# Taking the last norm's memory ahead of the general path's, and issuing its vector's load from SyncE

## The chip, the cores and the metric

The kernel runs on one core of a Trainium2 chip. A core has a matrix engine (PE), a vector engine (DVE), a scalar engine (ACT), GpSimd (POOL) and a sync engine (SP) that issues most of the DMAs here. Each engine takes its instructions strictly in the order in which they stand in its own queue, and waits for others on semaphores. The metric is the device time of one execution in microseconds (us): the median of three runs of the kernel before is 693.87 us (692.81 to 694.31).

## What is computed

One decoder block over 256 tokens of 1024 features: attention and a convolution side by side, cross-attention into a memory, and then a mixture of 32 experts and a last norm. Only the end matters here:

```
x = x + hierarchical_moe(h, ...)      # per token: the 2 best experts of the best group of 8
    # each expert: (silu(t @ w_gate) * (t @ w_up)) @ w_down, weighted and summed
return rmsnorm(x, final_g)            # x * rsqrt(mean(x*x) + eps) * final_g
```

`w_gate` and `w_up` are 1024 x 512 and `w_down` 512 x 1024 float32 for each of 32 experts: 192 MB that all have to come from memory.

## The kernel before

The experts are taken four at a time, in eight groups (`for g in range(NGR)`). Each expert has 32 slots for tokens (`CAP`), four experts fill 128 partitions, and each of the four quarters of PE's columns works for one expert. For a group PE gathers the tokens (L1034), multiplies with `w_gate` into `eg` and with `w_up` into `eu` (`two_rows`, L1310, where the loads are cut fine, otherwise L1339). Then `hidden_T` makes the hidden rows: ACT applies silu to `eg` (L1051), DVE multiplies with `eu` (L1052), PE turns the result over (L1055), ACT copies it to `hT` (L1058). Then PE multiplies with `w_down` into `ed`, and the result is spread back to the tokens and summed in the four banks `Y`.

Weights go through a ring of memory units of 8 KB per partition (`Ring`). `ring.queue` lists all loads in order ahead of time; `ring.done` gives units back and `ring.pump` then issues the next loads, from SP (L139). `ring.spare` hands out a unit for something that isn't a listed load.

An expert may get more than 32 tokens, so there is a general path, `overflow`: the engines read a count, and a loop handles the surplus where there is one. In these inputs the loop isn't entered. It has loads of its own into four spare units, `ow`. Every DMA of the program reports on one of eight semaphores (DMAHW0 to DMAHW7), used in turn and counted upwards, and the loop's loads count too. Where the loop isn't entered SP therefore goes another way (L1119): for six of the eight semaphores, one after another, it waits until the loads issued so far on it have landed, and then adds what the loop's load would have added.

The last group (g = 7) ends in `finale`. Its `w_down` is cut by rows of the experts, j = 0 to 3, and by columns, so that the last products wait for little data. In order of issue: (j = 0, in two pieces of 1 MB), then columns 0 to 511 of j = 1, 2, 3 (1 MB each), columns 512 to 1023 of j = 1, 2 (1 MB each), and columns 512 to 767 and 768 to 1023 of j = 3 (0.5 MB each). `SLICES` names the three column slices n = 0, 1, 2. `finale` is written out by hand for PE, ACT and DVE (`manual_schedule`): `down` and `down_c` are the products with `w_down` (L1179), `slots` copies them out of the banks (ACT, L1189), `spread` adds them to the tokens (PE, L1185), `begun` puts x itself into a bank (PE, L1173). The norm: `square` and `square_v` (ACT L1193, DVE L1198 and L1199) sum the squares into `junk`, DVE multiplies slice 0 by the vector `final_g` (L1249), `add_part` (DVE L1204), `root` (ACT L1207) and two reciprocals (DVE L1263, L1270) give the factor, `scaled` and `scaled_a` apply it (DVE L1212, ACT L1219), and two stores follow (L1222, one from SP and one from ACT).

Behind the last group's product with `w_gate` the code takes the general path (`overflow(*table)`), and behind that the memory for the end: `fin["g"]` for the vector `final_g`, loaded from ACT (L1346), `fin["Z"]` for the output and `fin["junk"]` for the squares. `close_sum` then finishes the right halves of the sums (L1163, L1164).

Of the kernel before, what the change touches and what calls it, by code (L numbers as in the profile page):

```python
# [21 lines left out]
P = 128  # L22
# [164 lines left out]
def body(tc, a, out):  # L187
    nc = tc.nc
# [808 lines left out]
    def e_ps(name, shape=(P, 512)):  # L997
        return ps2.tile(list(shape), F32, tag="e", name=name)
# [7 lines left out]
    def pick_mats(key_v, n, eng, SR=None):  # L1006

        w = n // CAP
        Sv = mo.tile([P, NT, n], F32, tag="S", name="S")
        if SR is None:  # L1010
            SR = mo.tile([P, NT, n], F32, tag="SR", name="SR")
        V.tensor_tensor(Sv.rearrange("p i (q c) -> p i q c", c=CAP),
                        iota1.unsqueeze(1).unsqueeze(1).to_broadcast([P, NT, w, CAP]),
                        key_v.unsqueeze(3).to_broadcast([P, NT, w, CAP]), op=OP.is_equal)
        A.activation(SR[:, 0], Sv[:, 0], AF.Copy, scale=r2[:, 0:1])  # L1015
        last_pick[0] = eng.tensor_scalar(SR[:, 1], Sv[:, 1], r2[:, 1:2], None, op0=OP.mult)  # L1016
        return Sv, SR

    def gate_mats(Sv, g_v, n):

        Sq = Sv.rearrange("p i (q c) -> p i q c", c=CAP)
        V.tensor_tensor(Sq, Sq, g_v.unsqueeze(3).to_broadcast([P, NT, n // CAP, CAP]), op=OP.mult)  # L1022
        return Sv
# [4 lines left out]
    def gather(SR, n, tg, j0=0, j1=NJ, step=4):  # L1028

        for ja in range(j0, j1, step):  # L1030
            t = e_ps("tgp", (P, step, n))
            for j in range(step):
                for i in range(NT):
                    T.matmul(t[:, j], X[:, i, ja + j::NJ], SR[:, i], start=i == 0, stop=i == NT - 1)  # L1034
            V.tensor_tensor(tg[:, ja:ja + step], t,  # L1035
                            gff[:, ja:ja + step].unsqueeze(2).to_broadcast([P, step, n]), op=OP.mult)

    def put_back(GS, n, GST=None):
        t = e_ps("GSp", (P, NT, P))
        for i in range(NT):  # L1040
            T.transpose(t[0:n, i], GS[:, i], ident)
        if GST is None:
            GST = mo.tile([n, NT, P], F32, tag="SR", name="GST")
        V.tensor_copy(GST, t[0:n])
        return GST
# [18 lines left out]
    def combine(pd, n, GST, yd, outs, w, first=False, last=False):  # L1064

        ins = A.copy(yd[:, :w], pd[0:n, :w])  # L1066
        for i in range(NT):
            T.matmul(outs[i], GST[:, i], yd[:, :w], start=first, stop=last)  # L1068
        return ins
# [45 lines left out]
    def overflow(ntot, eidx, thr):  # L1115

        ow, slots = zip(*[ring.spare((SLOT,)) for _ in range(4)])
        nv = nc.values_load(ntot[0:1, 0:1], min_val=0, max_val=NITEM)
        with tc.If(nv > 0):  # L1119
            with tc.For_i(0, nv, 1) as it_:  # L1120
                er = nc.values_load(eidx[0:1, ds(it_, 1)], min_val=0, max_val=NE - 1)
                kv = mo.tile([P, NT, 1], F32, tag="kc", name="okv")
                gv = mo.tile([P, NT, 1], F32, tag="gc", name="ogv")
                V.tensor_copy(kv, key[:, :, ds(er, 1)])
                V.tensor_copy(gv, GT[:, :, ds(er, 1)])
                V.tensor_tensor(kv, kv, thr[:, ds(it_, 1)].unsqueeze(1).to_broadcast([P, NT, 1]), op=OP.subtract)
                small_ = ow[2]
                Sv, SR = pick_mats(kv, CAP, G, small_[:, 0:NT * CAP].rearrange("p (i t) -> p i t", i=NT))
                tg = small_[:, 1280:1280 + NJ * CAP].rearrange("p (j t) -> p j t", j=NJ)
                gather(SR, CAP, tg)  # L1130
                GST = put_back(gate_mats(Sv, gv, CAP), CAP,
                               small_[0:CAP, 256:256 + NT * P].rearrange("p (i t) -> p i t", i=NT))
                pgu = []
                for w in (w_gate, w_up):
                    o = e_ps("oo")
                    for h in range(2):
                        wt_ = ow[h].rearrange("p (j f) -> p j f", j=4)
                        nc.sync.dma_start(wt_, w[ds(er, 1)].rearrange("o (p j) f -> p (o j) f", j=NJ)[:, 4 * h:4 * h + 4])
                        for jj in range(4):
                            j = 4 * h + jj  # L1140
                            T.matmul(o[0:CAP], tg[:, j], wt_[:, jj], start=j == 0, stop=j == NJ - 1,
                                     tile_position=(0, 0))
                    pgu.append(o)
                hh = hidden_T(pgu[0], pgu[1], CAP, small_[0:CAP, 512:512 + DE],
                              small_[:, 1024:1024 + 4 * CAP].rearrange("p (j t) -> p j t", j=4))
                yd = ow[3][0:CAP, 0:D].rearrange("p (n f) -> p n f", n=2)
                for n in range(2):
                    o = e_ps("od")
                    wt_ = ow[n].rearrange("p (j f) -> p j f", j=4)
                    nc.sync.dma_start(wt_, w_down[ds(er, 1)].rearrange("o (p j) n -> p (o j) n", j=4)[  # L1150
                        :, :, 512 * n:512 * n + 512])
                    for j in range(4):
                        T.matmul(o[0:CAP], hh[:, j], wt_[:, j], start=j == 0, stop=j == 3, tile_position=(0, 0))
                    combine(o, CAP, GST, yd[:, n], Ycols(512 * n, 512), 512)
        ring.done(*slots)


    fin = {}

    def close_sum():  # L1160

        for i in range(NT):
            T.matmul(Yp[i][1], ident, X[:, i, 512:], start=False, stop=True)  # L1163
            V.tensor_copy(X[:, i, 512:], Yp[i][1])  # L1164
# [158 lines left out]
    table = None  # L1323
    for g in range(NGR):
        tg, GS = state
        GST = put_back(GS, P) if g > 0 else None
        pgu = []
        for kind in ("eg", "eu"):
            o = e_ps(kind)
            if (kind, g) == ("eg", 0):  # L1330
                first_gate(o, tg)
            elif (kind, g) in FINE:
                for m in range(4):
                    two_rows(kind, g, m, o, tg)
            else:
                ws = [ring.take((kind, g, q)) for q in range(4)]
                for j in range(NJ):
                    for q in range(4):
                        T.matmul(o[32 * q:32 * q + 32], tg[:, j, 32 * q:32 * q + 32], ws[q][0][:, j],  # L1339
                                 start=j == 0, stop=j == NJ - 1, tile_position=(0, 32 * q))  # L1340
                ring.done(*[units for _, units in ws])
            pgu.append(o)
            if (kind, g) == ("eg", NGR - 1):
                overflow(*table)
                fin["g"] = ring.spare((D,))[0]
                nc.scalar.dma_start(fin["g"], a["final_g"].partition_broadcast(P))  # L1346
                fin["Z"] = ring.spare((NT, D))[0]
                fin["junk"] = ring.spare((NT, D))[0]
                close_sum()
        GST = GST or put_back(GS, P)  # L1350
        hh = hidden_T(pgu[0], pgu[1], P)
        last = g == NGR - 1
        if g == 1:

            for i in range(NT):
                T.matmul(Yp[i][0], ident, X[:, i, 0:512], start=False, stop=False)
        if last:
            finale(g, hh, GST)
            break
        yd = new_yd(P)  # L1360
        os_ = [e_ps("ed") for _ in range(2)]
        ws = [[ring.take(("ed", g, q, h)) for h in range(1 if q < 2 else 2)] for q in range(4)]
        for j in range(4):
            for n in range(2):
                for q in range(4):
                    w = ws[q][0][0][:, j] if q < 2 else ws[q][j // 2][0][:, j % 2]
                    T.matmul(os_[n][32 * q:32 * q + 32], hh[:, j, 32 * q:32 * q + 32], w[:, 512 * n:512 * n + 512],  # L1367
                             start=j == 0, stop=j == 3, tile_position=(0, 32 * q))
        ring.done(*[units for wq in ws for _, units in wq])
        for n in range(2):  # L1370
            combine(os_[n], P, GST, yd[:, n], Ycols(512 * n, 512), 512, g == 0, False)
        if g == 0:
            table = overflow_table()
        state = start_group(g + 1)
# [28 lines left out]
```

## Time and profile before

| | us |
|---|---|
| median of 3 runs | 693.87 (692.81 to 694.31) |
| the profiled execution: its own time | 692.93 |
| the profiled execution: its span, first to last instruction | 691.2 |
| PE busy | 574.6 (83%) |
| DVE busy | 223.4 (32%) |
| ACT busy | 173.3 (25%) |
| POOL busy | 119.0 (17%) |
| moved by DMA | 237.34 MB, mean 343 GB/s |

The profile is one execution. Times in its views are microseconds from the span's start; an instruction is named by engine, source line, operation and what it writes from what it reads. A "q" behind an engine's name (ACTq, SPq) means its instruction sequencer: waits and DMA issues, which don't count as busy. In brackets stands how long the engine was idle before, and what ended that.

### The profile page before, as it was taken

The page shows a single profiled execution, that of the slowest core. Times are in us where ns is not written, and L with a number is a line of the kernel's source. Part 1 is how long each engine was busy: PE and PEld are TensorE (multiplying, and loading weights), DVE is VectorE, ACT ScalarE, POOL GpSimd, SP SyncE. Part 2 cuts the span into 40 slices and gives each one's busy share as a digit, 9 for nine tenths or more (in the row PEclk, how much of TensorE's full clock was granted, in tenths as well). Part 3 has the DMA queues.
Part 4 walks back from the last instruction along what each step waited for, and adds up shares of the span by engine and source line. Part 5 has one row for each costly group of instructions (what it writes and reads, how often), then busy time and mean ns, then how long its engine had stood idle before and what let it go on. Part 6 is the DMA issues. An engine that isn't in the chain of part 4 may idle for free. (4 is left out here: it accounts for less than half of the span.)

```text
span 691.2 us, 8710 instructions
## 1 busy us (share of the span) xinstructions
PE 574.6 (83%) x3497; PEld 343.7 (50%) x3497; DVE 223.4 (32%) x488; ACT 173.3 (25%) x377; POOL 119.0 (17%) x106
## 2 busy tenths in 40 slices
PE   7999999998999999979767947967894795788726
PEld 4989889877998753615212501511250161234202
DVE  5799789887674710400000100000010010001002
ACT  6575765573555601000001000000000000000004
POOL 4556435673434100000000000000000000000000
PEclk9999999999999999999979968987996998799958
DMA  7999503554847899999999999999999999999981
GB/s 257 298 254 366 214 31 122 183 195 172 323 157 280 351 415 416 429 420 429 430 419 429 427 427 423 424 428 422 431 425 429 421 428 425 422 429 408 404 313 61
DMA packets 58730, 237.34 MB, mean 343 GB/s; under 512 B 10796, under 2 KB 30400, under 8 KB 46656
## 3 DMA queue, kind: packets, MB, share of 16 engines
q1 hardware_dynamic: 58400, 235.72, 86.0%
q10 hardware_dynamic: 288, 1.05, 0.4%
q8 instruction: 28, 0.46, 0.3%
q14 instruction: 14, 0.11, 0.0%
HBM read 235.70 MB, written 1.05 MB: 343 GB/s over the span
## 5 line engine op out<-in xcount | busy, mean ns | idle before, releaser
L433 POOL TENSOR_TENSOR WL<-w,WH 128x512 fp32r<-128x512 f32 (+1 forms) x80 | 109.1, 1373 | 109.8 <-ACT WH L431 98.8
L1339 PE MATMUL eu<-w,tg 128*32 128x512 f32 x448 | 82.2, 717 | 44.5 <-DMA w<-in_w_up 44.5
L1367 PE MATMUL ed<-w,hT 128*32 128x512 f32 x448 | 74.3, 659 | 23.4 <-DMA w<-in_w_down 18.6
L431 ACT CAST WH<-w 128x512 fp32r<-128x512 f32 (+1 forms) x120 | 72.9, 619 | 47.8 <-PE pmk L438 8.3
L1016 POOL TENSOR_SCALAR SR<-S,r 128x128 f32<-128x128 f32 x7 | 4.2, 604 | 387.9 <-PE Y L1068 337.0
L1339 PEld LDWEIGHTS eu<-w,tg 128*32 128x32 f32 x448 | 17.9, 127 | 104.5 <-DMA w<-in_w_up 63.9
L1034 PEld LDWEIGHTS tgp<-SR,X 128*128 128x128 f32 x256 | 62.0, 335 | 12.0 <-ACT SR L1015 9.5
L1034 PE MATMUL tgp<-SR,X 128*128 128x128 f32 x256 | 63.8, 406 | 3.6 <-ACT SR L1015 3.6
L1052 DVE TENSOR_TENSOR sgm<-sgm,eu 128x512 f32<-128x512 f32 x8 | 5.5, 687 | 182.1 <-PE eu L1339 168.4
L534 DVE SCALAR_TENSOR_TENSOR cacc<-z,pT,cacc 128x256 f32<-128x256 f32 x116 | 56.4, 486 | 2.6
L1367 PEld LDWEIGHTS ed<-w,hT 128*32 128x32 f32 x448 | 19.1, 115 | 73.6 <-issue 41.1
L1339 PE MATMUL eg<-w,tg 128*32 128x512 f32 x384 | 50.4, 614 | 4.1 <-DMA w<-in_w_gate 4.1
L1058 ACT COPY hT<-hTp 128x512 f32<-128x512 f32 x8 | 4.7, 586 | 161.2 <-PE hTp L1055 129.2
L1022 DVE TENSOR_TENSOR S<-S,GT 128x256 f32<-128x256 f32 x8 | 3.4, 425 | 122.3 <-POOL SR L1016 122.2
L433 DVE TENSOR_TENSOR WL<-w,WH 128x512 fp32r<-128x512 f32 (+1 forms) x40 | 36.4, 912 | 10.7 <-ACT WH L431 10.4
L1051 ACT ACTIVATE sgm<-eg 128x512 f32<-128x512 f32 x8 | 4.8, 597 | 135.2 <-PE eg L1339 85.6
L1339 PEld LDWEIGHTS eg<-w,tg 128*32 128x32 f32 x384 | 12.9, 112 | 37.1 <-issue 27.6
L1066 ACT COPY yd<-ed 128x512 f32<-128x512 f32 x14 | 8.2, 586 | 89.6 <-PE ed L1367 89.6
L1035 DVE TENSOR_TENSOR tg<-tgp,g_norm_ffn_g 128x512 f32<-128x512 f32 (+2 forms) x19 | 11.5, 607 | 53.0 <-PE tgp L1034 53.0
L1068 PE MATMUL Y<-yd,GST 128*128 128x512 f32 x56 | 25.9, 605 | 0.0
L1179 PE MATMUL ed<-w,hT 128*32 128x256 f32 (+1 forms) x96 | 9.2, 534 | 14.8 <-ACT hT L1058 14.8
L437 PE MATMUL pmk<-w,WH 128*128 128x256 f32 x64 | 18.7, 293 | 0.0
(354 smaller groups left out, 1005.3 us busy)
## 6 DMA issues: line engine op xcount, KB each, us to landing
w<-in_w_up SPq DMA_DIRECT2D x28, 2048.0 KB, 34.3
w<-in_w_gate SPq DMA_DIRECT2D x24, 2048.0 KB, 29.5
w<-in_w_down SPq DMA_DIRECT2D x35, 1024.0 KB, 31.5
w<-in_w_down SPq DMA_DIRECT2D x14, 2048.0 KB, 28.9
w<-in_w_gate SPq DMA_DIRECT2D x16, 1024.0 KB, 14.0
w<-in_w_mkv SPq DMA_DIRECT2D x8, 1024.0 KB, 12.9
w<-in_w_up SPq DMA_DIRECT2D x8, 1024.0 KB, 29.7
w<-in_w_in SPq DMA_DIRECT2D x7, 1024.0 KB, 7.3
```

The lines of the kernel that those rows point to most:

```text
L431: A.copy(hi, src)
L433: (V if nsplit[0] % 3 == 0 else G).tensor_tensor(lo, src, hi.bitcast(F32), op=OP.subtract)
L437: T.matmul(o, L[0], R[0], start=first, stop=False)
L534: V.scalar_tensor_tensor(dst, z[:, cb, t:t + S], pT[:, 4 * t + cb:4 * t + cb + 1], acc, op0=OP.mult, op1=OP.add)
L1034: T.matmul(t[:, j], X[:, i, ja + j::NJ], SR[:, i], start=i == 0, stop=i == NT - 1)
L1035: V.tensor_tensor(tg[:, ja:ja + step], t, gff[:, ja:ja + step].unsqueeze(2).to_broadcast([P, step, n]), op=OP.mult)
L1052: V.tensor_mul(sg, sg, pu[0:n])
L1066: ins = A.copy(yd[:, :w], pd[0:n, :w])
L1068: T.matmul(outs[i], GST[:, i], yd[:, :w], start=first, stop=last)
L1179: T.matmul(os_[n][32 * q:32 * q + 32, :w], hh[:, j, 32 * q:32 * q + 32], wq(q), start=j == 0, stop=j == 3, tile_position=(0, 32 * q))
L1339: T.matmul(o[32 * q:32 * q + 32], tg[:, j, 32 * q:32 * q + 32], ws[q][0][:, j], start=j == 0, stop=j == NJ - 1, tile_position=(0, 32 * q))
L1367: T.matmul(os_[n][32 * q:32 * q + 32], hh[:, j, 32 * q:32 * q + 32], w[:, 512 * n:512 * n + 512], start=j == 0, stop=j == 3, tile_position ...
```

## The change

`overflow(*table)` moves from ahead of the three `ring.spare` calls to behind them, and the load of `final_g` goes from ACT's queue to SP's:

```diff
             if (kind, g) == ("eg", NGR - 1):
-                overflow(*table)
                 fin["g"] = ring.spare((D,))[0]
-                nc.scalar.dma_start(fin["g"], a["final_g"].partition_broadcast(P))
+                nc.sync.dma_start(fin["g"], a["final_g"].partition_broadcast(P))
                 fin["Z"] = ring.spare((NT, D))[0]
                 fin["junk"] = ring.spare((NT, D))[0]
+                overflow(*table)
                 close_sum()
```

So the three units are taken from those that are free before the general path takes its four, and none of them is a unit into which the general path loads. The load's line becomes L1345.

On ACT, where the general path's branch (L1119) is behind it and `hidden_T` of the last group comes next (`hT` is the hidden rows, `hTp` the bank they come from; DMAHW0 to 7 are the DMAs' semaphores, the number behind them is a serial number of the program):

```order
 L1119 UNCONDITIONAL_BRANCH [waits Activation_49,Activation_sequencer_49]
-L1346 DMA w<-in_final_g 128x1024 [waits DMAHW2_49,DMAHW4_49,DMAHW0_49,PE_49]
 L1058 COPY hT<-hTp 128x512 [waits DVE_49,PE_49]
 L1189 COPY yd<-ed 128x512 [waits PE_49,Activation_49]
 L1240 ACT_TABLE_LOAD
```

The load, with its waits for three DMA semaphores, is gone from the place ahead of the copy to `hT`; the copy's own waits are for DVE and PE alone, in both kernels.

On SP, at the end of the list of loads and ahead of the read of the general path's count (`ntot`):

```order
 L139 DMA w<-in_w_down 128x4x256 [waits DMAHW2_49]
 L139 DMA w<-in_w_down 128x4x256 [waits DMAHW3_49]
+L1345 DMA w<-in_final_g 128x1024 [waits DMAHW4_49]
 L1118 TENSOR_LOAD ntot [waits DVE_49]
 L1119 COMPARE_AND_BRANCH
```

The load now stands behind the last two pieces of `w_down` and ahead of the branch, and waits for one semaphore, the one that it will report on itself: DMAHW4, used last by the load eight places before it.

On DVE, where the last norm begins (the first read of `final_g`, which is `w` here):

```order
 L1052 TENSOR_TENSOR sgm<-sgm,eu 128x512 [waits DVE_49,PE_49,Activation_49]
-L1249 TENSOR_TENSOR w<-Y_3019,w 128x512 [waits DMAHW2_49,DMAHW4_49,DMAHW0_49,Activation_49]
+L1249 TENSOR_TENSOR w<-Y_3019,w 128x512 [waits DMAHW4_49,DMAHW2_49,DMAHW7_49,DMAHW1_49,Activation_49]
 L1249 TENSOR_TENSOR w<-Y_3021,w 128x512 [waits Activation_49]
 L1204 SCALAR_TENSOR_TENSOR fpart<-fss,eps_t 128x1 x2
```

The order is the same; the multiplication waits for the vector in both kernels (DMAHW4), and for earlier users of its output's unit, which is another one now. PE's and POOL's orders are the same in both kernels.

## Rows read from the trace of the kernel before

**Rows 1.** The page: span, and the DMA engines' busy share in 40 slices
```profile
span 691.2 us, 8710 instructions
...
DMA  7999503554847899999999999999999999999981
```

**Rows 2.** The chain that ended last, window 640 to 692 (start, length, what)
```profile
668.82 0.04 ACTq L1346
...
670.02 3.64 PE ed L1179 x24
```

**Rows 3.** Timeline of ACT, 600 to 692
```profile
636.79 0.60 ACT L1051 ACTIVATE sgm<-eg 128x512 f32<-128x512 f32 x1 [18.09 <-PEq L1119]
...
669.38 0.59 ACT L1058 COPY hT<-hTp 128x512 f32<-128x512 f32 x1 [31.99 <-DMA w<-in_w_down]
```

**Rows 4.** Line L1346 alone: count, durations in ns, first and last start
```profile
L1346 ACTq EVENT_SEMAPHORE  x2: 17/28/38, 637.7 to 668.8; - x2
...
DMA to landing us min/median/max: 4.0/4.0/4.0
```

**Rows 5.** Line L1119 on SP, in windows 663.1 to 666.5 and 668 to 668.73
```profile
L1119 SPq EVENT_SEMAPHORE  x2: 17/17/17, 663.5 to 666.0; - x2
...
L1119 SPq EVENT_SEMAPHORE  x1: 17/17/17, 668.7 to 668.7; - x1
```

**Rows 6.** Timeline of PE, 640 to 692
```profile
654.53 0.64 PE L1055 MATMUL hTp<-ident,sgm 128*128 128x128 f32 x4
670.02 3.64 PE L1179 MATMUL ed<-w,hT 128*32 128x512 f32 x24 [14.85 <-ACT hT L1058]
673.59 1.11 PE L1173 MATMUL yl<-X,ident 128*128 128x256 f32 x2
674.63 3.65 PE L1179 MATMUL ed<-w,hT 128*32 128x512 f32 x40
678.20 1.98 PE L1185 MATMUL Y<-yd,GST 128*128 128x512 f32 x4
...
680.55 1.93 PE L1179 MATMUL ed<-w,hT 128*32 128x256 f32 x32
```

**Rows 7.** Line L139 on SP, window 636.5 to 638.8: one load of `w_down`
```profile
L139 SPq DMA_DIRECT2D w<-in_w_down x1: 2308/2308/2308, 636.5 to 636.5; - x1
...
DMA to landing us min/median/max: 18.6/18.6/18.6
```

**Rows 8.** DMA by queue (q1 SP, q10 ACT), windows 670:671, 671:672, 672:673
```profile
q1 hardware_dynamic: 128, 0.12, 38.7%
...
q10 hardware_dynamic: 74, 0.27, 76.0%
q1 hardware_dynamic: 3, 0.00, 0.7%
...
q10 hardware_dynamic: 16, 0.03, 7.6%
```

**Rows 9.** Timeline of SP, 560 to 692
```profile
634.16 28.21 SPq L139 DMA_DIRECT2D w<-in_w_down  x9
```

**Rows 10.** Stretches: PE, PEld, DVE, ACT, POOL busy, PEclk, DMA share, GB/s
```profile
657.00:670.00 13.00, 0.00 (x0) 0.00 (x0) 0.00 (x0) 0.59 (x1) 0.00 (x0) 0.51 0.99 356
670.00:674.00 4.00, 3.98 (x25) 1.40 (x26) 0.00 (x0) 0.00 (x0) 0.00 (x0) 0.50 0.46 162
674.00:688.00 14.00, 10.48 (x88) 4.72 (x87) 4.59 (x15) 7.14 (x18) 0.00 (x0) 0.98 0.06 25
```

**Rows 11.** Timeline of DVE, 637 to 692
```profile
680.15 1.49 DVE L1249 TENSOR_TENSOR w<-Y,w 128x512 f32<-128x512 f32 x2 [26.08 <-ACT w L1193]
681.55 0.22 DVE L1204 SCALAR_TENSOR_TENSOR fpart<-fss,eps_t 128x1 f32<-128x1 f32 x2
683.79 0.16 DVE L1204 SCALAR_TENSOR_TENSOR fpart<-fss,fpart 128x1 f32<-128x1 f32 x1 [2.02 <-ACT w L1193]
```

## The prediction, made before the changed kernel ran

> **What bounds the kernel now.** I read the DMA share in slices first: from the middle of the span to its last two slices the DMA engines are 90% busy or more [rows 1], so most of the kernel runs at the rate at which weights arrive, and nothing in this change moves those bytes. What is left to win is what stands behind the last weights. The chain that ended last is read next, from its front: it doesn't begin with a weight that PE waits for, but with ACT's wait ahead of the load of `final_g`, and then PE starts on `w_down` at 670.02 [rows 2]. So I looked at what ACT did before. It finished silu of the last group at 636.79 + 0.60 = 637.4, its sequencer met the first wait of L1346 at 637.7 and the second ended at 668.8 [rows 3, 4]. ACT takes its queue in order, so the copy to `hT` stood behind that wait. PE had the hidden rows turned over at 654.53 + 0.64 = 655.17, and then sat idle for 14.85 us until the copy, at 669.38, had ended [rows 3, 6].
>
> What did L1346 wait for? The order rows name DMAHW2, DMAHW4 and DMAHW0. The unit for `final_g` is one into which the general path may load, so the count that L1346 wants includes that path's loads, which SP adds on its way round the loop. SP can begin with that only when all weights are issued, at 634.16 + 28.21 = 662.4 [rows 9], and it goes through the semaphores one by one: it passed DMAHW0 at 666.0 and DMAHW1 at 668.7 [rows 5], then the rest at once. DMAHW0 to 3 belong to the last four loads, so these two times are also the landings of columns 512 to 1023 of j = 1 and of j = 2.
>
> **The change, part by part.**
>
> *Memory ahead of the general path.* The three units now come from the free ones, and the general path loads into none of them. The copy to `hT` has nothing ahead of it but the branch, and waits for DVE and PE only. It starts at 655.17 + 0.04 and takes 0.59 [rows 3], so PE can begin at 655.9 instead of 670.02: 14.1 us earlier. How much of that reaches the end depends on what is late next, and there are three candidates.
>
> (a) The data. The first piece of j = 0 has landed before the second, which lands at 636.5 + 18.6 = 655.1 [rows 7]; from there to 666.0 lie four more 1 MB loads, 2.7 us apart. PE's price for them: 24 instructions in 3.64 us are two products over 512 columns (j = 0, all three slices) at half clock, 40 instructions in 3.65 us are four such products at full clock [rows 6, 10], so one costs 0.91 us at full and 1.82 at half clock. Both fit into 2.7 us. The work that ran from 670.02 to 677.4 before (j = 0, slice 0 of j = 1 to 3) is hidden behind the loads at either clock: j = 0, `begun` and three products take 3.64 + 1.11 + 5.46 = 10.2 us at half clock, 655.9 + 10.2 = 666.1. The data of the last slices end at about 671.1: SP's queue moved 0.12 MB between 670 and 671 and three packets after that [rows 8]. The last quarter of the 32 instructions (1.93 / 4 = 0.48) then ends at 671.6, where it ended at 680.55 + 1.93 = 682.48 before. By that alone the end comes 10.9 us earlier, at a span of 680.3.
>
> (b) `final_g`, now behind `w_down` in SP's queue. Before, it was issued at 668.9 and landed 4.0 us later, at 672.9 [rows 4], and nobody waited: DVE reads it at 680.15 [rows 11]. Now DVE needs it at about 671. Its issue takes between 0.38 us (ACT's, L1346) and 2.3 us (a load of `w_down` on SP [rows 7]); SP has only the loop test and the store behind it, so that costs nothing, and it is in the queue by 665. It is then moved behind the last weights. Its own bytes were still moving at 672 (0.27 MB in 671:672, 0.03 MB in 672:673 [rows 8]); in one queue they follow the weights without a gap, so the whole can be a little earlier than 672.9 but not earlier than the weights' end, 671.1. The near row is 672.9, and I take 672.6. From the first multiplication to the third L1204 DVE needs 1.49 + 0.22 less their overlap, 681.77 - 680.15 = 1.62 us; before it then waited until 683.79 for ACT [rows 11]. From 683.79 on DVE and ACT take turns without a pause to the end of the span, 691.2 - 683.79 = 7.4. So 672.6 + 0.05 + 1.62 + 7.4 = 681.7.
>
> (c) PE's clock. It was at half (1.2 GHz) while PE idled from 657 to 670, stayed there for the first 4 us of work, and was full (2.4 GHz) after that [rows 10]. With the change PE works in short pieces between landings from 656 to 666, so I can't say which level it has then. From 666.0 on the rest doesn't pause: one product, `spread` of slice 0, `begun` and four half products. Before, this and three more products ran from 674.63 to 682.48 at full clock [rows 6, 10], so it is 7.85 - 3 x 0.91 = 5.1 us. If the first 4 us of it run at half, as before, they do 2 us worth, and the other 3.1 end at 673.1; the end then lies 691.2 - 682.48 = 8.7 later, at 681.8. If the clock comes back 4 us later still (674), the rest ends at 675.1 and the span at 683.8.
>
> The Trainium skill (TensorE: Matmul & The Clock Gate, section HAM oscillation) says that a kernel whose matmuls wait for DMA between short pieces falls back to the slow clock again and again. That speaks against getting all of (a). The trace agrees in that PE's idle stretch and the 4 us behind it were at half clock [rows 10].
>
> (b) and (c) end within 0.2 us of each other and don't add, since DVE waits for the later of them. I take 681.8, that is 9.4 us less than 691.2.
>
> *Output and squares in other units.* Z and `junk` lie where the weights of the last `eg` were, which PE had read by 637. Their writers start after 668, so the waits are over by then: nothing.
>
> *SP's way round the loop* starts up to 2.3 us later and now waits for DMAHW2 in place of DMAHW4. Its followers are the store at 686 and nothing else: nothing.
>
> **The rivals.**
>
> *Half clock to the end.* If the pieces between 656 and 666 leave PE at half clock and it never comes back, 5.1 us of work take 10.2, to 676.2, and the two last `spread`s (before, from 682.48 to the next DVE step at 683.79 and some way on) cost about 1.6 more: 676.2 + 8.7 + 1.6 = 686.5, 4.7 us saved. For it: half clock in all of 657 to 674. Against: 4 us without a pause brought the clock back before [rows 10].
>
> *Neither clock nor vector binds.* If the clock stays full and the vector lands by 671.2, case (a) is left: 680.3. Against: the vector's 0.5 MB are still moving at 672.
>
> *The vector drowns in SP's queue, slower than before.* A load of `w_down` took 18.6 us from issue to landing on this queue [rows 7]. If `final_g`, issued at 662.4, took that too, it would land at 681.0 and the span would be 681.0 + 9.1 = 690.1. The point from which it costs is a landing at 682.1, 19.7 us after issue; at 24 us the span would be 695.5. Against: 18.6 us is a full queue's backlog, and here the weights ahead of it are through at 671.1.
>
> *It is only another queue.* The engine that issues a load may not matter: then only the 0.38 us of ACT's issue [rows 2, 3] go, and the copy stays late, 690.8. Against it stands that ACT waited for 31 us and issued for 0.38. The Trainium skill (DMA: Bandwidth & Descriptors, section Issuing engines are not separate DMA queues) has this rule: loads from any engine share the same 16 DMA engines, and another issuer saves only its issue time. It speaks of the transfers; the trace has its loss in the queue ahead of the transfer.
>
> **How the numbers follow.** The sum was made on the profiled execution, 692.93 us with a span of 691.2; it lies 0.9 below the median of the three runs. Taking the savings off the median, 693.87: forecast 9.4 saved, 684.5, chance 0.68 (with the clock's return 4 us later, 7.4 saved, 686.5, inside it); neither binds, 10.9 saved, 683.0, 0.14; half clock to the end, 4.7 saved, 689.2, 0.12; only another queue, 693.5, 0.04; slower, 0.02 and above 694. The range 682.7 to 687.5 takes in the first two, with some 0.3 us at the low end and 1 us at the high end for the spread of runs, and leaves out the last three. A measurement of this kernel tells 0.2% (1.4 us) from no change; so faster 0.94, same 0.04, slower 0.02.
>
> **What would show it.** Right: ACT's copy to `hT` at 655, without a DMA ahead of it; PE's products with `w_down` waiting for DMA, the last at 671; `final_g` landed near 672.6 and DVE's first L1249 right behind it. Wrong: a copy to `hT` that still starts behind 660; a `final_g` landing after 675; a half-clock stretch that reaches past 676; or a last weight that lands after 672.

## The result, and the profile after

The changed kernel takes 684.61 us (median of 4 runs, 683.42 to 684.92), the kernel before 693.71 us with one more run beside it. The ratio is 0.9867, 95% interval 0.985 to 0.9884: 9.1 us less. 684.5 us and 9.4 us less were forecast.

The chain that ended last, in the changed kernel (start, length, what), no longer begins with ACT. It answers to [rows 2]:

```profile
653.19 13.97 DMA w<-in_w_down
667.16 0.04 issue
667.21 1.94 PE ed L1179 x16
```

PE now begins the last stretch where a weight lands, at 667.2, and not where ACT lets it. ACT's timeline around the copy to `hT`, which answers to [rows 3]:

```profile
637.97 0.60 ACT L1051 ACTIVATE sgm<-eg 128x512 f32<-128x512 f32 x1 [16.39 <-PEq L1119]
654.88 0.58 ACT L1058 COPY hT<-hTp 128x512 f32<-128x512 f32 x1 [16.31 <-PE hTp L1055]
```

The copy follows PE's turning over; no load and no DMA's wait stands between. PE's timeline of the end, which answers to [rows 6] (in brackets how long PE was idle, and what ended it):

```profile
655.52 2.80 PE L1179 MATMUL ed<-w,hT 128*32 128x512 f32 x24 [0.68 <-ACT hT L1058]
658.25 0.70 PE L1173 MATMUL yl<-X,ident 128*128 128x256 f32 x2
659.10 1.06 PE L1179 MATMUL ed<-w,hT 128*32 128x512 f32 x8 [0.16 <-DMA w<-in_w_down]
661.78 1.07 PE L1179 MATMUL ed<-w,hT 128*32 128x512 f32 x8 [1.62 <-DMA w<-in_w_down]
664.50 1.92 PE L1179 MATMUL ed<-w,hT 128*32 128x512 f32 x8 [1.65 <-DMA w<-in_w_down]
667.21 1.94 PE L1179 MATMUL ed<-w,hT 128*32 128x256 f32 x16 [0.79 <-DMA w<-in_w_down]
669.07 3.12 PE L1185 MATMUL Y<-yd,GST 128*128 128x512 f32 x4
672.03 0.59 PE L1173 MATMUL yl<-X,ident 128*128 128x256 f32 x2
672.55 1.93 PE L1179 MATMUL ed<-w,hT 128*32 128x256 f32 x32
```

The one wait of 14.85 us has become short ones: 0.68 us for the copy itself, then four, each ended by the landing of a piece of `w_down`. From 667.21 on PE doesn't pause, and it is slow at first: `spread` takes 3.12 us where it took 1.98 before. The same stretches by windows (PE, PEld, DVE, ACT, POOL busy, then the granted clock as a share of 2.4 GHz, DMA share, GB/s) answer to [rows 10]:

```profile
655.00:664.50 9.50, 5.56 (x43) 1.52 (x43) 0.00 (x0) 0.46 (x1) 0.00 (x0) 1.00 1.04 385
664.50:671.40 6.90, 6.11 (x27) 1.96 (x28) 0.00 (x0) 2.08 (x3) 0.00 (x0) 0.51 1.00 352
671.40:681.60 10.20, 5.08 (x44) 2.76 (x42) 4.50 (x15) 5.05 (x16) 0.00 (x0) 1.00 0.34 134
```

DVE's timeline, which answers to [rows 11], the end of ACT's square, and the load of `final_g` on its line:

```profile
674.27 1.29 DVE L1249 TENSOR_TENSOR w<-Y,w 128x512 f32<-128x512 f32 x2 [20.29 <-DMA w<-in_final_g]
675.47 0.22 DVE L1204 SCALAR_TENSOR_TENSOR fpart<-fss,eps_t 128x1 f32<-128x1 f32 x2
675.79 0.16 DVE L1204 SCALAR_TENSOR_TENSOR fpart<-fss,fpart 128x1 f32<-128x1 f32 x1
...
675.56 0.20 ACT L1193 ACTIVATION_READ_ACCUMULATOR w<-Y 128x1 f32 x1
...
L1345 SPq DMA_DIRECT2D w<-in_final_g x1: 2581/2581/2581, 663.6 to 663.6; - x1
...
DMA to landing us min/median/max: 10.5/10.5/10.5
```

DVE waits for the vector, issued at 663.56 and landed 10.5 us later, at 674.0. The third L1204 starts at 675.79. DVE's own steps behind the vector ended at 675.47 + 0.22 = 675.69, and ACT's square for which it also waits, the last of PE's path, at 675.56 + 0.20 = 675.76. So the vector and PE's products come out within 0.1 us of each other.

One thing is needed to compare traces: they don't all reach the last group at the same time. What lies ahead of the change scatters by about a microsecond from execution to execution (the close of the sums starts between 637.5 and 638.7 in three traces of the changed kernel), so stretches are measured below from the close of the sums, PE's L1163, to the end of the span. Its row in the kernel before and in the changed kernel:

```profile
637.00 1.96 PE L1163 MATMUL Y<-X,ident 128*128 128x512 f32 x4 [0.30 <-PEq L1119]
...
638.17 1.95 PE L1163 MATMUL Y<-X,ident 128*128 128x512 f32 x4 [0.30 <-PEq L1119]
```

Before it is 691.2 - 637.0 = 54.2 us, now 683.2 - 638.2 = 45.0 us: 9.2 less.

### The profile page after: what moved, and what is told of

Its sections match the earlier page's. It is cut to its first block, busy times and chain, and to the rows that moved or that the text cites. A ratio compares the mean times of both kernels' runs of the same rounds, so it can differ in the third digit from the quotient of the medians.

```text
span 683.2 us, 8708 instructions
## 1 busy us (share of the span) xinstructions
PE 574.3 (84%) x3497; PEld 344.2 (50%) x3497; DVE 223.5 (33%) x488; ACT 173.2 (25%) x377; POOL 118.9 (17%) x106
## 5 line engine op out<-in xcount | busy, mean ns | idle before, releaser
L1339 PE MATMUL eg<-w,tg 128*32 128x512 f32 x384 | 48.7, 595 | 4.1 <-DMA w<-in_w_gate 3.9
L433 DVE TENSOR_TENSOR WL<-w,WH 128x512 fp32r<-128x512 f32 (+1 forms) x40 | 36.4, 912 | 11.0 <-ACT WH L431 10.7
L437 PE MATMUL pmk<-w,WH 128*128 128x256 f32 x64 | 18.7, 292 | 0.0
L438 PE MATMUL pmk<-w,WH 128*128 128x256 f32 x64 | 18.7, 292 | 0.0
```

What stands on the lines that cost most here:

```text
L433: (V if nsplit[0] % 3 == 0 else G).tensor_tensor(lo, src, hi.bitcast(F32), op=OP.subtract)
L437: T.matmul(o, L[0], R[0], start=first, stop=False)
L438: T.matmul(o, L[0], R[1], start=False, stop=False)
```

## Experiments: which part of the change brings it

The change moves the memory, the place of the load and its queue at once. Three kernels take these apart.

**act_early**: memory and load ahead of the general path, but the load from ACT.

```diff
-                nc.sync.dma_start(fin["g"], a["final_g"].partition_broadcast(P))
+                nc.scalar.dma_start(fin["g"], a["final_g"].partition_broadcast(P))
```

> The changed kernel with the vector's load issued from ACT, not SP. The memory is taken ahead of the general path; the load then stands on ACT ahead of the second last group's combining copies, far ahead of the branch, so it moves among the weights of the last group. Theory 'what counts is that nothing that waits for the general path's loads stands ahead of the copy to hT': the copy starts at about 655 as in the changed kernel, the vector has long landed, the last weights land 1.2 us later (0.5 MB at 410 GB/s), so 684 to 685 us. Theory 'the queue counts: the load has to leave ACT': ACT is held again, about 693 us.

Measured: 685.46 us, a little above the 684 to 685 expected; ratio to the kernel before 0.9881 (0.9861 to 0.9901). ACT's timeline, then the window of PE's half clock and DVE's third L1204:

```profile
602.36 0.58 ACT L1058 COPY hT<-hTp 128x512 f32<-128x512 f32 x1 [22.85 <-PE hTp L1055]
612.96 0.38 ACTq L1345 DMA_DIRECT2D w<-in_final_g  x1
614.70 0.59 ACT L1066 COPY yd<-ed 128x512 f32<-128x512 f32 x1 [11.76 <-PE ed L1367]
...
655.85 0.58 ACT L1058 COPY hT<-hTp 128x512 f32<-128x512 f32 x1 [16.28 <-PE hTp L1055]
...
664.50:671.40 6.90, 5.16 (x26) 1.64 (x27) 0.00 (x0) 1.87 (x2) 0.00 (x0) 0.51 0.98 349
...
676.26 0.16 DVE L1204 SCALAR_TENSOR_TENSOR fpart<-fss,fpart 128x1 f32<-128x1 f32 x1 [2.01 <-ACT w L1193]
```

Nothing ties the load to the last group once its memory is free, so it went out one group earlier. ACT was held for it too, from 602.9 to 613.0, but there the next step on ACT waits for PE until 614.7 anyway. The copy to `hT` is free at 655.85, and nearly the whole gain is there, from ACT: the close of the sums lies later, at 639.17, and from there to the end it is 683.7 - 639.2 = 44.5 us. So the load doesn't have to leave ACT.

**act_behind**: memory ahead of the general path, the load on ACT behind it. One column of the unit is first written by DVE behind the branch, which keeps the load there.

```diff
-                nc.sync.dma_start(fin["g"], a["final_g"].partition_broadcast(P))
                 fin["Z"] = ring.spare((NT, D))[0]
                 fin["junk"] = ring.spare((NT, D))[0]
                 overflow(*table)
                 close_sum()
+                V.tensor_copy(fin["g"][:, 0:1], X[:, NT - 1, 512:513])
+                nc.scalar.dma_start(fin["g"], a["final_g"].partition_broadcast(P))
```

> Memory ahead of the general path as in the changed kernel, but the load on ACT and behind the branch (one column of the vector's unit is written by DVE behind the branch, so that the load can't move ahead of it). The load's memory has nothing to do with the general path's; but it reports on DMAHW4 and waits for that semaphore at a count that SP adds to on its way round the loop. Theory 'memory': the copy to hT starts at about 655, 685 us. Theory 'the turn in the semaphores': ACT waits until SP has gone through DMAHW0, 1 and 4, at about 669, the copy starts there and the time is that of the kernel before, 693 to 694 us.

Measured: 692.74 us, ratio 0.9987 (0.9975 to 1.0). ACT's timeline, the load's line, and SP's way round the loop:

```profile
638.05 0.60 ACT L1051 ACTIVATE sgm<-eg 128x512 f32<-128x512 f32 x1 [18.09 <-PEq L1119]
670.17 0.38 ACTq L1350 DMA_DIRECT2D w<-in_final_g  x1
670.66 0.58 ACT L1058 COPY hT<-hTp 128x512 f32<-128x512 f32 x1 [32.01 <-DMA w<-in_w_down]
...
DMA to landing us min/median/max: 3.9/3.9/3.9
...
L1119 SPq EVENT_SEMAPHORE  x7: 17/17/17, 664.7 to 670.3; - x7
```

The memory has nothing to do with the general path's any more, and ACT is held just as long: it goes on at 670.17, while SP ends its way, at 670.3. In the program of this kernel the wait for DMAHW0 has gone with the memory. What is left is the load's own turn on DMAHW4 (and an old count on DMAHW2): SP adds the general path's share to DMAHW4 behind DMAHW0 and DMAHW1. In the kernel before both waits stood there, and the turn on DMAHW4 ended last: SP passed DMAHW0, which the memory asks for, at 666.0 [rows 5], and ACT went on at 668.8 [rows 4]. Moving the memory alone, with the load on ACT behind the branch, brings nothing that can be told.

**sp_behind**: the kernel before, with the load on SP and nothing else.

```diff
-                nc.scalar.dma_start(fin["g"], a["final_g"].partition_broadcast(P))
+                nc.sync.dma_start(fin["g"], a["final_g"].partition_broadcast(P))
```

> The kernel before with the vector's load on SP and nothing else changed: memory behind the general path's, load behind the branch on SP. Theory 'what counts is that ACT isn't held': the copy to hT starts at about 655; SP issues final_g when it has gone round the loop, at about 669 to 670, it lands 4 us later, at 673 to 674, and the time is 684.5 to 685.5 us. Theory 'both parts of the change are needed': 690 us or more.

Measured: 685.27 us, ratio 0.9878 (0.9854 to 0.9902); 45.0 us from the close of the sums, as with the whole change. ACT's copy, and the load's line:

```profile
656.52 0.58 ACT L1058 COPY hT<-hTp 128x512 f32<-128x512 f32 x1 [17.88 <-PE hTp L1055]
...
L1346 SPq DMA_DIRECT2D w<-in_final_g x1: 357/357/357, 670.6 to 670.6; - x1
...
DMA to landing us min/median/max: 3.6/3.6/3.6
```

SP issues the vector 7.1 us later than in the changed kernel, and it lands at 674.3 in place of 674.0, since the weights were ahead of it in either case. One changed word brings, by the trace, the whole gain; the medians of 685.27 and 684.61 us can't be told apart. What counts is that no wait for SP's way round the loop stands on ACT ahead of the copy; the load may go to SP, or early enough on ACT.

The Trainium skill (DMA: Bandwidth & Descriptors, section Issuing engines are not separate DMA queues) says that loads from any engine run on the same DMA engines. For the transfer these traces agree: 3.9 us from ACT and 3.6 us from SP. The two kernels issue the vector within 0.5 us of each other (670.17 and 670.65); the 7.5 us between their times lie in what is queued behind the waiting issuer.

## Experiments: what is late next

The forecast rested on two things that were to end within 0.2 us of each other: the vector, and PE at half clock. If that is so, taking either away brings nothing, and taking both away brings something.

The changed kernel was timed again beside them:

> The changed kernel once more, beside the three kernels that change one of its last waits. Both theories expect 684.6 us (684.0 to 685.1), 9.1 us less than the kernel before.

Measured: 684.2 us (684.16 to 685.5), 45.0 us from the close of the sums.

**no_vector**: the load left out, x's rows in its place (`final_g` isn't applied).

```diff
                 fin["g"] = ring.spare((D,))[0]
-                nc.sync.dma_start(fin["g"], a["final_g"].partition_broadcast(P))
+                fin["g"] = X[:, 0]
```

> The changed kernel without the load of final_g: the last norm multiplies by the first rows of x in place of final_g, so the 0.5 MB at the end of SP's queue and the wait for them are gone. In the changed kernel DVE's first multiplication waits for the vector (landed 674.04) and the step behind it starts at 675.79, 0.04 us after ACT's square, which waits for PE (clock half until 671.4), ended. Theory 'both bind at the same time' and theory 'only PE's clock binds': 684.3 to 684.8 us, since PE's products still end near 674.5. Theory 'only the vector binds': 683.0 us, 1.6 less, since PE's last product could end 0.5 us after the last weights.

Measured: 684.68 us (681.76 to 686.69); 683.7 - 638.5 = 45.2 us from the close of the sums. DVE's timeline:

```profile
672.18 0.69 DVE L1249 TENSOR_TENSOR w<-Y,X 128x512 f32<-128x512 f32 x1 [16.27 <-ACT w L1193]
673.37 0.69 DVE L1249 TENSOR_TENSOR w<-Y,X 128x512 f32<-128x512 f32 x1 [0.50 <-ACT w L1193]
673.98 0.22 DVE L1204 SCALAR_TENSOR_TENSOR fpart<-fss,eps_t 128x1 f32<-128x1 f32 x2
676.22 0.16 DVE L1204 SCALAR_TENSOR_TENSOR fpart<-fss,fpart 128x1 f32<-128x1 f32 x1 [2.02 <-ACT w L1193]
```

DVE is through with the multiplications 2 us early and then waits these 2 us for ACT's square, that is for PE. No gain.

**pe_busy**: the vector as in the changed kernel, and PE filled between the landings with products of ones. One `begun` moves behind them, since it shares their bank.

```diff
+            warm_bank = e_ps("yl")
-            outs = [Ycols(0, 512), [begun(1, i, Yp[i][1]) for i in range(NT)], [begun(2, 0, e_ps("yl"))]]
+            outs = [Ycols(0, 512), [begun(1, i, Yp[i][1]) for i in range(NT)], []]
...
             for j in (1, 2, 3):
                 down_c(j, 0)
+                warm(11)      # 11 products of ones, 256 columns, bf16, into warm_bank
+            outs[2].append(begun(2, 0, warm_bank))
```

> The changed kernel with 11 small products of ones (256 columns) on PE behind each of j = 1, 2, 3 of the first column slice, into a bank that begun uses later; they fill PE's idle stretches of 1.6 us between landings. Expected of the clock: full from about 658 to the end. Theory 'both bind' and theory 'only the vector binds': 684.3 to 684.8 us, since DVE still waits for final_g until about 674. Theory 'only PE's clock binds': 683.0 us, PE's last product ending at 672.8, 0.5 us after the last weights, in place of 674.5.

Measured: 684.57 us (684.34 to 684.87); 683.1 - 638.45 = 44.7 us from the close of the sums. Windows, then the timelines of PE and DVE:

```profile
655.00:664.50 9.50, 7.64 (x63) 3.20 (x62) 0.00 (x0) 0.59 (x1) 0.00 (x0) 1.00 1.04 386
664.50:671.40 6.90, 6.66 (x55) 3.33 (x59) 0.00 (x0) 3.25 (x6) 0.00 (x0) 1.00 1.03 362
...
668.48 1.98 PE L1186 MATMUL Y<-yd,GST 128*128 128x512 f32 x4
670.30 0.59 PE L1174 MATMUL yl<-X,ident 128*128 128x256 f32 x2
670.82 1.57 PE L1180 MATMUL ed<-w,hT 128*32 128x256 f32 x24
673.11 0.64 PE L1180 MATMUL ed<-w,hT 128*32 128x256 f32 x8 [0.71 <-DMA w<-in_w_down]
...
674.55 1.29 DVE L1259 TENSOR_TENSOR w<-Y,w 128x512 f32<-128x512 f32 x2 [20.32 <-DMA w<-in_final_g]
...
676.01 0.16 DVE L1205 SCALAR_TENSOR_TENSOR fpart<-fss,fpart 128x1 f32<-128x1 f32 x1
```

The clock is full throughout, `spread` takes 1.98 us again, and PE now waits 0.71 us for the very last weights. It doesn't help: DVE still waits for the vector until 674.5. The Trainium skill (TensorE: Matmul & The Clock Gate, section HAM oscillation) warns of pauses for DMA between short pieces; these windows agree, with 0.51 between 664.5 and 671.4 in the changed kernel and 1.00 here.

**no_vector_pe_busy**: both edits (again without applying `final_g`).

> Both edits together: no load of final_g (x's first rows in its place, so the output is scaled wrongly) and the small products that fill PE's idle stretches. Theory 'both bind at the same time': 682.7 to 683.1 us, 1.7 us less, though each edit alone brings nothing. Theory 'only the clock binds': as with the small products alone. Theory 'only the vector binds': as with the vector's load left out alone.

Measured: 684.4 us (682.62 to 684.6), above the 682.7 to 683.1 expected; the medians can't tell it from the others, since the execution's way to the last group scatters by as much. From the close of the sums, at 638.97, it is 682.8 - 639.0 = 43.8 us, against 45.0, 45.2 and 44.7. DVE's timeline, PE's last products with `w_down`, and what SP's queue still moved between 673.0 and 673.1 (after that, nothing):

```profile
672.34 0.22 DVE L1205 SCALAR_TENSOR_TENSOR fpart<-fss,eps_t 128x1 f32<-128x1 f32 x2
675.38 0.16 DVE L1205 SCALAR_TENSOR_TENSOR fpart<-fss,fpart 128x1 f32<-128x1 f32 x1 [2.81 <-ACT w L1194]
...
673.56 0.64 PE L1180 MATMUL ed<-w,hT 128*32 128x256 f32 x8 [0.72 <-DMA w<-in_w_down]
...
q1 hardware_dynamic: 2, 0.00, 4.0%
```

The third L1204 (here L1205) starts 36.4 us behind the close of the sums, in the changed kernel 37.6, with either edit alone 37.7 and 37.6. So the trace shows that both had to go; 1.2 us come of it, where 1.7 were expected.

`act_early`, above, is one more kernel whose vector lands long ahead. It takes 44.5 us from the close of the sums, its third L1204 starts 37.1 us behind it, and DVE waits 2.01 us there for ACT's square. Its half clock lies where the changed kernel's does, 664.5 to 671.4, but its last stretch on PE starts at 668.18 in place of 667.21, so less of it runs slowly. Taking the vector's wait alone away thus brings between -0.2 and 0.5 us, by where the half clock meets the work.

**small_load** and **small_load_pe_busy**: a way to get this in a whole kernel. `final_g` comes as 4 KB at the kernel's start, and PE spreads it over the partitions.

```diff
-                nc.sync.dma_start(fin["g"], a["final_g"].partition_broadcast(P))
...
+    nc.sync.dma_start(g8, a["final_g"].rearrange("(k p) -> k p", k=NJ))
...
+    def spread_gain():
+        for n in range(2):
+            t = e_ps("gb")
+            for k in range(4):
+                T.matmul(t[:, k * P:(k + 1) * P], ident[0:NJ, 4 * n + k:4 * n + k + 1].to_broadcast([NJ, P]), g8,
+                         start=True, stop=True)
+            V.tensor_copy(fin["g"][:, 512 * n:512 * n + 512], t)
...
                 close_sum()
+                spread_gain()
```

> A version that should beat the changed kernel only together with a busy PE: final_g comes as 4 KB at the kernel's start (8 partitions of 128 numbers), and PE spreads it over the partitions with eight small products at the start of the last group's eu, DVE copies it to the unit. The 0.5 MB at the end are gone. Theory 'both bind at the same time': 684.2 to 684.8 us, no gain, since PE is still at half clock. Theory 'only the vector binds': 683.0 us.

Measured: 684.15 us, ratio 0.9871 (0.9851 to 0.9891); 682.1 - 637.0 = 45.1 us from the close of the sums. No gain alone. With the products of `pe_busy` added, and the changed kernel a third time on the same chip:

> The changed kernel again, on the same chip as the version below: 684.2 to 684.6 us; from the start of the sums' close (PE's products with x, at about 638) to the end of the span 45.0 us, as in the two traces before.

> A whole version for both waits at once: final_g as 4 KB at the start, spread by PE, and the small products that keep PE busy between landings. Theory 'both bind at the same time': from the close of the sums to the end 43.8 us in place of 45.0, as with both waits taken away before, so 683.0 to 683.6 us; by the medians that is at the edge of what can be told. Theory 'neither matters, the runs only scatter': 45.0 us from the close of the sums and 684.4 us.

Measured: the changed kernel 684.35 us (683.96 to 685.58), ratio 0.987 (0.9853 to 0.9886), 683.8 - 638.7 = 45.1 us from the close of the sums; with both edits 682.87 us (681.36 to 684.31), ratio 0.9851 (0.9829 to 0.9874), 680.9 - 637.1 = 43.8 us. The intervals overlap, so by the times alone it is not shown to be faster than the changed kernel; its one trace has the gain, 45.1 against 43.8 us, in the same place as before:

```profile
669.49 1.50 PE L1190 MATMUL ed<-w,hT 128*32 128x256 f32 x24
671.72 0.64 PE L1190 MATMUL ed<-w,hT 128*32 128x256 f32 x8 [0.73 <-DMA w<-in_w_down]
```

PE has done all it can and waits for the last half megabyte: now the data bind.

## Why the prediction was right, point by point

To set it beside the forecast, 1.2 us are taken off times of the changed kernel's trace, by which its close of the sums lies later.

- *ACT's wait goes, the copy starts at 655.* Right: 654.88, of which the 1.2 make 653.7. The earlier end of `eu` did it: its last products ran at full clock here, 1.91 us in place of 3.2. That is hidden behind the loads: a later trace of the changed kernel has 3.48 us there and also ends 45.1 us behind the close of the sums.
- *The pieces up to j = 3 are hidden behind their loads at either clock.* Right: PE waited 1.6 us for two of them.
- *(b) the vector lands at 672.6, third L1204 at 674.3.* It landed at 674.0 - 1.2 = 672.8 and the step came at 674.6, 0.3 late. Its issue took 2.58 us, above the upper bound given, 2.3, and cost nothing, as said.
- *(c) the first 4 us at half clock, the last products with `w_down` end at 673.1.* They ended at 674.48 - 1.2 = 673.3. The forecast left open which clock PE has between 656 and 666: it was full until 664.5, then half until 671.4, which is 670.2 in the forecast's frame, and 670 was assumed. That PE would be at half when the last stretch began was taken over from the trace of before, where PE had idled for 14.85 us; here it had worked at full clock until 2.7 us before. That the sum came out is luck to that extent: with the half clock 1 us earlier against the work, as in `act_early`, PE's part is 0.5 us shorter.
- *They tie.* Right, by the two-by-two of experiments: the vector's wait alone -0.2 to 0.5 us, PE's clock alone 0.3, both together 1.2. It was the step with the least margin: nothing in the trace of before showed that 672.6 and 673.1 with their tails would meet, only the sum did.
- *(a) by the data alone, 10.9 us less.* Mis-sized by 0.5: the two kernels without either wait measure 54.2 - 43.8 = 10.4. The step that failed was to let the last products start where the last packets ended, 671.1. In `no_vector_pe_busy`, where nothing follows the weights in the queue, the last two packets lie between 673.0 and 673.1, which is 671.1 in the frame of before, and PE starts at 673.56, 0.5 us later. The last quarter then took 0.64 us, not 0.48; some 0.1 us came back in the steps behind it.
- *The memory ahead of the general path frees ACT.* This step of the explanation was wrong in its cause, though the sum didn't suffer. It put ACT's wait down to the unit into which the general path may load, and the freeing to the new memory. That wait was there, but it ended at 666.0, and the load's turn on DMAHW4 at 668.8; `act_behind` has the new memory and the old time. Nor is the new memory needed: with the load on SP, the old memory does as well (`sp_behind`). It helps only in that the load may then go out ahead of the branch.
- *Z and `junk` elsewhere, SP's way round the loop: nothing.* Right: no first writer waits for a DMA other than the vector's.
- *Rivals.* Half clock to the end: no, it came back at 671.4. The vector drowns: it took 10.5 us from issue to landing, where 19.7 was the point. Only another queue: no, far more than the issue's 0.38 us went; yet the other queue alone is enough (`sp_behind`), since nothing that others wait for stands behind the load there. Neither binds: not in the changed kernel, only with both waits taken away.

## What to carry to other kernels

An issue of a DMA is an instruction with waits, and on an engine that also computes, everything behind it pays for them; look in the order for DMAs with several semaphores ahead of a step that others wait for. Where loads share a few semaphores in turn, a load waits for strangers too, and moving its memory doesn't change that. When two late things end within some tenths of a microsecond, test them together as well as one by one, or each will look as if it didn't matter.

## What the runs showed of the hardware

- PE's clock at the end depends on what it did in between: with products of 1.06 us and pauses of 1.6 us from 659 to 664 it fell to half from 664.5 to 671.4; with the same pauses mostly filled it stayed full (windows above). Filling cost nothing, since PE only waited there: the products behind start 29.0 us behind the close of the sums in both kernels.
- SP's issue of a load takes as long as one of `w_down` (2.58 us) where it stands right behind the weights, and 0.36 us once they are through, for the same 0.5 MB.
- The same 0.5 MB landed at 674.0 when queued behind the weights at 663.6 and at 674.3 when issued at 670.6.
